# Weight sums and split feed-forward weights made beside the state space, one step per gate product, and GpSimd's sums moved to VectorE

## The chip, the core and the metric

The kernel runs on one core of a Trainium2 chip. Time is the device time of one execution, in microseconds (us). Five engines work from queues of their own, each in order: TensorE (PE in the profile; its weight loads are PEld), VectorE (DVE), ScalarE (ACT), GpSimd (POOL) and SyncE (SP), which only issues DMAs here. An instruction waits for semaphores, and everything behind it on its engine waits with it.

## What is computed

One decoder block over 1024 tokens of width 1024, in float32, with two branches, a mixer, a cross-attention into 256 memory tokens, and a feed-forward network of hidden width 2816:

```python
u = rms_norm(h, norm_mix[l])
proj = u @ w_in[l]
u_ssm, q, k, v, f_logit, gate_logits = jnp.split(proj, [...], axis=-1)
y_ssm = jax.nn.gelu(s5_ssm(u_ssm, ...))
glu_a, glu_b = jnp.split(y_ssm @ w_glu[l], 2, axis=-1)
out_a = glu_a * jax.nn.sigmoid(glu_b)
out_b = forgetting_attention(q, k, v, f_logit + b_forget[l]) @ w_fox_o[l]
gate_a, gate_b = jnp.split(jax.nn.sigmoid(gate_logits), 2, axis=-1)
h = h + (gate_a * out_a + gate_b * out_b) @ w_mix_out[l]
h = h + memory_cross_attention(rms_norm(h, norm_mem_q[l]), ...)
f_a, f_b = jnp.split(rms_norm(h, norm_ffn[l]) @ w_ffn_in[l], 2, axis=-1)
h = h + (jax.nn.silu(f_a) * f_b) @ w_ffn_out[l]
return rms_norm(h, norm_final)
```

## The kernel before

**Precision.** A float32 product is made of three products in fp32r: each operand is split into a high part (a cast by ScalarE) and a low part (source minus high, by VectorE, or by GpSimd where a flag says so). `split` (L175 to L178) does it; so casts stand at L177 and low parts at L178 for all callers.

**Seven products.** The mixer's product and the feed-forward products use a scheme of the Strassen kind on 2 x 2 blocks: seven block products in place of eight, at the price of sums and differences of blocks of both operands. The names S1 to S4, A11, A12 and A22 are such operands of the activations (h or l behind the name: high or low part); sums_d and w_d hold sums of weight blocks in DRAM.

**Stages, in the order of the span.** Up to about 115 us: load, normalise, transpose and project. About 117 to 330 us (`stage_ssm`): the state space, in four quarters q, among 32 gate products `gate(j, h)` of 24 matmuls each. A gate product ends in a sigmoid by ScalarE, and `mark` keeps these sigmoids. A dictionary `todo` says which step of the state space or of the mixer's weights stands ahead of which gate product; the program's order and a scheduler that looks at the queues make the order of each engine. For each quarter `xg` is read back from u_d, transposed data that the quarter's first products read; it is issued by SyncE, and so are the loads of raw weights, the stores y_d and the reads back of Ts. The block sums of w_mix_out are made here too (`mix_fetch`, `mix_sums`, `mix_store`, L490 to L505): two loads of 128x1024, four VectorE sums, four stores to sums_d, four times. About 330 to 620 us: the forgetting attention. About 620 to 820 us: the gated unit, `fox_part`, then the mixer's product (`mix_mm`, L615, and `mix_add`, L622, which adds a PSUM bank into the residual h on VectorE; the bank is free for its next product after that). Beside the mixer, a list `side` of small steps is worked off, one at a time: reads of S4, and the functions of `ahead(j)` for the feed-forward's first two weight blocks, j=0 and 1 (AHEAD_IN). `ahead` fetches 2 x 512 KB of w_ffn_in into wpr, makes five sums per block on GpSimd (L693 to L698), splits (wph, wpl), and stores seven tiles of 512 KB per block to w_d from ScalarE's queue (L671). About 820 to 945 us: cross-attention. From about 928 us: `norm_blocks(t)`, eight times, which normalises a token tile (the multiplier by `rstd`: VectorE, GpSimd, VectorE, L192 to L202), scales it into xs (L216, one buffer), transposes it on TensorE (L222) and, for t from 4 to 7, makes the operands S1 to S4 with the tile t-4 that it reads back from x_d as xa: two differences on VectorE (L877, L878), two on GpSimd (L879, L880), then splits, those of S2 with the low part on GpSimd. r_d keeps what makes S4 and A22 later. Then the feed-forward network: its input products (L961) from about 950 to 1395 us, the output products (L1098) from 1400 us.

`B.tc.issue_after(x)` makes the instructions of its body that run on the same engine as x, here ScalarE, come behind x in order.

## Time and profile before

| | us |
|---|---|
| median of three executions | 1608.38 (1606.6 to 1611.47) |
| the profiled execution | 1612.03 |
| its span | 1610.3 |
| its mean granted TensorE clock | 0.979 of full |

| engine | busy us | share |
|---|---|---|
| PE | 1539.8 | 96% |
| PEld | 1265.1 | 79% |
| DVE | 1071.1 | 67% |
| ACT | 670.9 | 42% |
| POOL | 282.9 | 18% |

The profile shows one execution. A row of the timeline or of the waits has the start in the span, the duration, the engine (SPq and ACTq: a DMA issue), the line, the operation, what it writes and reads, the shape, and in brackets how long the engine sat idle before it and what ended that. The DMA engines carry 161 GB/s on average, and 381 GB/s in the busiest of forty slices.

### The profile page before, as it was taken

To read this page: it belongs to the slowest core of one execution; us is meant where nothing else is said; L and a number is where in the kernel's file an instruction comes from. 1 tells how busy PE (TensorE), PEld (TensorE's weight loads), DVE (VectorE), ACT (ScalarE), POOL (GpSimd) and SP (SyncE) were. 2 spreads that over 40 slices of the span, in tenths; PEclk is the share of its full clock that TensorE was granted. 3 is DMA by queue.
4 is the path that set the end of the run, shared out by engine and by line. 5 is a ranking of instruction groups with operands and counts; after the bars stand their busy time and mean duration, and the time that the engine had idled before them with its cause. 6 is when DMAs were issued, how large, how long until landed. Compare 5 with 4: busy or idle time off the path is not lost.

```text
span 1610.3 us, 20551 instructions
## 1 busy us (share of the span) xinstructions
PE 1539.8 (96%) x7301; PEld 1265.1 (79%) x7301; DVE 1071.1 (67%) x1870; ACT 670.9 (42%) x1191; POOL 282.9 (18%) x353
## 2 busy tenths in 40 slices
PE   6899899999999899999899989999999999999997
PEld 5688788898777668887688767888888888788886
DVE  5758656434687777779665697677667776465555
ACT  5522333423566553233455564333333333244342
POOL 3024444010121124122202231001000000000001
PEclk8999999999999999999999999999999999999999
DMA  8747654552032736567632177444544454797642
GB/s 263 149 99 177 226 139 93 126 165 30 2 67 45 177 83 195 184 214 273 219 129 68 53 268 248 155 152 157 164 163 150 158 166 147 256 381 227 195 157 105
DMA packets 202871, 258.71 MB, mean 161 GB/s; under 512 B 36024, under 2 KB 127064, under 8 KB 202256
## 3 DMA queue, kind: packets, MB, share of 16 engines
q1 hardware_dynamic: 196144, 241.67, 50.2%
q10 hardware_dynamic: 6624, 15.73, 2.5%
q8 instruction: 57, 0.93, 0.2%
q14 instruction: 46, 0.38, 0.1%
HBM read 176.08 MB, written 83.20 MB: 161 GB/s over the span
## 4 chain that ended last, share of the span: by engine, by line
PE 76%; DVE 8%; DMA 5%; POOL 4%; issue 3%; ACT 2%; SPq 1%; DVEq 0%; POOLq 0%; ACTq 0%
PE mm L961 14%; PE pv L961 7%; PE mm L167 7%; PE mm L168 7%; PE mm L169 7%; PE mm L1098 4%; PE sc L961 3%; PE sc L1098 3%; PE pv L1098 3%; PE sc L167 2%; PE sc L169 2%; PE sc L168 2%; PE misc L1098 1%; DMA or<-in_w_ffn_out_dram 1%; PE pv L615 1%
## 5 line engine op out<-in xcount | busy, mean ns | idle before, releaser
L178 DVE TENSOR_TENSOR wlo<-raw,whi 128x1024 fp32r<-128x1024 f32 (+2 forms) x126 | 136.5, 1085 | 118.2 <-ACT whi L177 117.7
L177 ACT CAST whi<-raw 128x1024 fp32r<-128x1024 f32 (+2 forms) x127 | 115.6, 914 | 150.4 <-PE mm L168 41.7
L167 PE MATMUL mm<-uh,whi 128*128 128x512 f32 x344 | 138.2, 402 | 1.9 <-ACT whi L177 1.9
L178 DVE TENSOR_TENSOR ol<-or,oh 128x1024 fp32r<-128x1024 f32 x73 | 89.3, 1224 | 71.9 <-ACT oh L177 70.9
L169 PE MATMUL mm<-uh,wlo 128*128 128x512 f32 x344 | 136.1, 396 | 0.5 <-DVE wlo L178 0.5
L168 PE MATMUL mm<-ul,whi 128*128 128x512 f32 x344 | 135.8, 395 | 0.0
L177 ACT CAST oh<-or 128x1024 fp32r<-128x1024 f32 x73 | 76.8, 1052 | 104.5 <-PE mm L1098 34.8
L993 POOL TENSOR_TENSOR g<-a,c 128x512 f32<-128x512 f32 x22 | 35.6, 1616 | 381.6 <-ACT a L992 381.6
L1725 POOL TENSOR_TENSOR pl<-pf,ph 128x512 fp32r<-128x512 f32 (+1 forms) x32 | 39.5, 1235 | 225.8 <-DVE ph L1724 180.8
L169 PEld LDWEIGHTS mm<-uh,wlo 128*128 128x128 f32 x344 | 65.5, 190 | 15.0 <-DVE wlo L178 1.5
L167 PEld LDWEIGHTS mm<-uh,whi 128*128 128x128 f32 x344 | 65.8, 191 | 14.4 <-ACT whi L177 2.3
L168 PEld LDWEIGHTS mm<-ul,whi 128*128 128x128 f32 x344 | 65.6, 191 | 10.9
L196 POOL TENSOR_TENSOR r<-ms,mhalf 128x1 f32<-128x1 f32 (+1 forms) x30 | 20.5, 684 | 296.8 <-DVE ms L192 269.8
L1722 ACT ACTIVATE pf<-sc 128x512 f32<-128x512 f32 (+1 forms) x96 | 46.4, 490 | 49.6 <-DVE sc L1718 30.0
L961 PE MATMUL pv<-S3h,we 128*128 128x512 f32 x176 | 58.0, 391 | 1.1 <-ACT S3h L177 1.1
L1728 DVE TENSOR_TENSOR pl<-pf,ph 128x512 fp32r<-128x512 f32 (+2 forms) x64 | 35.6, 558 | 11.4 <-ACT ph L1727 10.7
L1193 POOL TENSOR_TENSOR sg<-sg,ga 128x512 f32<-128x512 f32 x16 | 28.4, 1801 | 73.2 <-DVE sg L1186 56.5
L167 PE MATMUL sc<-uh,whi 128*128 128x512 f32 x104 | 41.3, 397 | 0.0
L1098 PE MATMUL mm<-oh 128*128 128x512 f32 x106 | 41.2, 389 | 0.0
L1098 PE MATMUL mm<-ol,oh 128*128 128x512 f32 x106 | 41.2, 389 | 0.0
L1098 PE MATMUL mm<-oh,ol 128*128 128x512 f32 x106 | 41.2, 389 | 0.0
L167 PE MATMUL mm<-yh,whi 128*128 128x512 f32 x104 | 41.0, 394 | 0.0
(680 smaller groups left out, 4643.8 us busy)
## 6 DMA issues: line engine op xcount, KB each, us to landing
or<-c_d SPq DMA_DIRECT2D x77, 256.0 KB
wo<-in_w_ffn_out_dram SPq DMA_DIRECT2D x22, 512.0 KB
c_d<-g SPq DMA_DIRECT2D x44, 256.0 KB
t_d<-wo SPq DMA_DIRECT2D x44, 256.0 KB
or<-t_d SPq DMA_DIRECT2D x44, 256.0 KB
raw<-in_w_ffn_in_dram SPq DMA_DIRECT2D x20, 512.0 KB
rawb<-in_w_ffn_in_dram SPq DMA_DIRECT2D x20, 512.0 KB
raw<-in_w_in_dram SPq DMA_DIRECT2D x18, 512.0 KB
```

The lines of the kernel that those rows point to most:

```text
L167: T.matmul(ps, lh, rh, start=first, stop=False)
L168: T.matmul(ps, lh, rl, start=False, stop=False)
L169: T.matmul(ps, ll, rh, start=False, stop=last)
L177: self.A.copy(hi, src)
L178: (self.G if pool_lo else self.V).tensor_sub(lo, src, f32(hi))
L961: T.matmul(ps, l_[:, k, :], r_, start=first and k == 0 and i == 0, stop=k == 3 and i == 2, skip_group_check=True)
L993: G.tensor_mul(g[:, 512:], a1, c1)
L1098: T.matmul(ps, l_[:, gi], r_[:, 512:], start=n < 3 and p == 0 and k == 0 or n == 7 and p == 0 and k == 0, stop=p == NP - 1 and k == 2, ski ...
L1193: self.B.G.tensor_mul(self.out[j][:, cs], self.out[j][:, cs], ga)
L1722: self.exp = A.activation(pf[:, off:], ps[:, off:], AF.Exp)
L1725: G.tensor_sub(pl[:, off:], pf[:, off:], f32(ph[:, off:]))
L1728: V.tensor_sub(pl[:, off:], pf[:, off:], f32(ph[:, off:]))
```

## The change

It has five parts.

1. Tiles that prepare the state space come from the pool `sp` and no longer from `xin`, which is released when the first stage ends.
2. The split feed-forward weights of j=0 and 1 are made in `stage_ssm`. Each step is a job bound behind one gate product's sigmoid: the fetch at gate 15 + 8j, the seven parts at gates 16 + 8j to 22 + 8j in the order 1, 2, 5, 6, 7, 3, 4, and the stores of a part one gate later. Tiles are `wk` (128x1024, two buffers, shared with the mixer's sums) and `wh` (128x512, three buffers). Sums are on VectorE, and the stores to w_d go out from SyncE's queue, 14 of 256 KB per block.
3. The mixer's weight sums are such jobs too: fetch, sums and stores at gates 3 + 3k, 4 + 3k and 5 + 3k.
4. In `fox_part` the second difference of xm moves from GpSimd to VectorE, and S1 is split at once and no longer later (`late`). `side` keeps only the reads of S4.
5. In `norm_blocks` both sums and the low parts of S2 move from GpSimd to VectorE, S2 is put ahead of S3 and S1, and the sign of what r_d holds is turned, so that S4 needs no negation.

```diff
+    V, mw, kept = B.V, {}, {}
+    def wide():
+        return [qp.tile([P, D], F32, tag="wk", bufs=2, name="wk") for _ in range(2)]
...
+    def ffn_fetch(j):
+        mw["f", j] = wide()
+        for w_, c in zip(mw["f", j], (0, FH)):
+            S.dma_start(w_.rearrange("p (k c) -> p k c", k=8),
+                        w_ffn_in[:, c + j * P:c + (j + 1) * P].rearrange("(k p) c -> p k c", p=P))
+
+    def ffn_part(j, n):
+
+        (a1, a2), (b1, b2) = [(w_[:, :512], w_[:, 512:]) for w_ in mw["f", j]]
+        src, adds = {1: (a1, ()), 2: (a2, ()), 5: (a1, ((a2, b2), (a1, b1), (b1, b2))), 6: (a1, ((a2, a1), (a1, b2))),
+                     7: (b1, ()), 3: (b2, ()), 4: (a2, ())}[n]
+        for o, i in adds:
+            V.tensor_add(o, o, i)
+        kept[j, n] = [qp.tile([P, 512], F32R, tag="wh", bufs=3, name="wh") for _ in range(2)]
+        B.split(*kept[j, n], src)
+
+    def ffn_keep(j, n):
+        i, h = {1: (0, 0), 2: (0, 1), 5: (2, 0), 6: (2, 1), 7: (4, 0), 3: (5, 0), 4: (5, 1)}[n]
+        for m, t_ in enumerate(kept.pop((j, n))):
+            o = 512 * (m if n == 7 else h)
+            S.dma_start(w_d[j, i + (m if n != 7 else 0)][:, o:o + 512], f32(t_))
+
+    jobs = {}
+    for k in range(4):
+        for i, f in ((3 + 3 * k, mix_fetch), (4 + 3 * k, mix_sums), (5 + 3 * k, mix_store)):
+            jobs.setdefault(i, []).append(lambda f=f, k=k: f(k))
+    for j in range(AHEAD_IN):
+        jobs.setdefault(15 + 8 * j, []).append(lambda j=j: ffn_fetch(j))
+        for i, n in enumerate((1, 2, 5, 6, 7, 3, 4)):
+            jobs.setdefault(16 + 8 * j + i, []).append(lambda j=j, n=n: ffn_part(j, n))
+            jobs.setdefault(17 + 8 * j + i, []).insert(0, lambda j=j, n=n: ffn_keep(j, n))
...
-    for k in range(4):
-        for i, f in ((10 + 5 * k, mix_fetch), (12 + 5 * k, mix_sums), (13 + 5 * k, mix_store)):
-            todo.setdefault(i, []).append(lambda f=f, k=k: f(k))
...
         f()
+        if i in jobs:
+            with B.tc.issue_after(mark[-1].ins):
+                for g in jobs.pop(i):
+                    g()
...
-            if h and late:
-                late.pop(0)()
...
-        G.tensor_sub(x_[:, 512:], s1, x_[:, 512:])
+        V.tensor_sub(x_[:, 512:], s1, x_[:, 512:])
...
-        late.append(lambda: give("S1", bslot, k, x_[:, 512:]))
+        give("S1", bslot, k, x_[:, 512:])
...
-    side = [f for j in range(AHEAD_IN) for f in ahead(j)]
-    side[:0] = late + [lambda kk=kk: mix_s4(kk) for kk in range(2)]
+    side = [lambda kk=kk: mix_s4(kk) for kk in range(2)]
...
-        G.tensor_sub(a11, s1n, a11)
-        G.tensor_add(a12, a11, a12)
+        V.tensor_sub(a11, s1n, a11)
+        V.scalar_tensor_tensor(out=a12, in0=a11, scalar=-1.0, in1=a12, op0=ALU.mult, op1=ALU.subtract)
+        put("S2", slot, i, a11)
         put("S3", bslot, i, s3)
         put("S1", bslot, i, s1n, neg=True)
-        put("S2", slot, i, a11, low=G)
...
-        put("S4", bslot, i, y[:, :512], neg=True)
+        put("S4", bslot, i, y[:, :512])
```

What the engines' orders look like then is shown at three places; a row has the line, the operation, what it writes and reads, and the shape.

First SyncE in the second quarter of the state space, around the load of xg for q=1. Before:

```order
L505 DMA sums_d<-mw 128x512 x4
L492 DMA mw<-in_w_mix_out_dram 128x1024 x2
L153 DMA raw<-in_w_in_dram 128x4x256 x2
L505 DMA sums_d<-mw 128x512 x4
L1449 DMA xg<-u_d 128x1024
L1508 DMA y_d<-yh 128x1024
L1508 DMA y_d<-yl 128x1024
```

And with the change:

```order
L511 DMA sums_d<-wk 128x512 x4
L498 DMA wk<-in_w_mix_out_dram 128x1024 x2
L153 DMA raw<-in_w_in_dram 128x4x256 x2
L511 DMA sums_d<-wk 128x512 x4
L516 DMA wk<-in_w_ffn_in_dram 128x8x128
L1429 DMA xg<-u_d 128x1024
L516 DMA wk<-in_w_ffn_in_dram 128x8x128
L1488 DMA y_d<-yh 128x1024
L1488 DMA y_d<-yl 128x1024
```

A fetch of w_ffn_in now stands ahead of xg and another behind it; the mixer's sums keep their place.

Second VectorE in the mixer's product, where h is the residual (one name per token tile), raw and whi/wlo a mixer weight and its parts. Before:

```order
L622 TENSOR_TENSOR h_6963<-h_6963,mm 128x512
L178 TENSOR_TENSOR wpl<-wpr,wph 128x1024
L622 TENSOR_TENSOR h_6964<-h_6964,mm 128x512
L622 TENSOR_TENSOR h_6965<-h_6965,mm 128x512
L178 TENSOR_TENSOR wpl<-wpr,wph 128x512
L178 TENSOR_TENSOR wlo<-raw,whi 128x1024
L178 TENSOR_TENSOR wpl<-wpr,wph 128x512
L622 TENSOR_TENSOR h_6966<-h_6966,misc 128x512
L178 TENSOR_TENSOR wph<-wpr,wph 128x512
L622 TENSOR_TENSOR h_6959<-h_6959,mm 128x512
```

With the change, the same token tiles:

```order
L659 TENSOR_TENSOR h_7068<-h_7068,mm 128x512
L659 TENSOR_TENSOR h_7069<-h_7069,mm 128x512
L659 TENSOR_TENSOR h_7070<-h_7070,mm 128x512
L178 TENSOR_TENSOR wlo<-raw,whi 128x1024
L659 TENSOR_TENSOR h_7071<-h_7071,misc 128x512
L178 TENSOR_TENSOR wlo<-raw,whi 128x1024
L659 TENSOR_TENSOR h_7064<-h_7064,mm 128x512
L192 TENSOR_SCALAR ms_7339<-ss 128x1
L200 TENSOR_TENSOR rt_7341<-r_7340 128x1
```

The splits of the feed-forward weights are gone from between the additions; a chain for a multiplier (ms, r, rt) follows the first of the last four additions.

Third VectorE in the norm blocks of t=5 to 7 (s, sx: the differences; xs: the scaled tile; S1l, S2l, S3l: low parts). Before:

```order
L877 TENSOR_TENSOR s_8962<-xa,misc 128x512
L216 SCALAR_TENSOR_TENSOR xs<-h_6965,r_9024,gbc 128x1024
L878 TENSOR_TENSOR sx<-misc,sx 128x512
L178 TENSOR_TENSOR S3l<-s_8962,S3h 128x2x128 x2
L856 SCALAR_TENSOR_TENSOR S1l<-sx,S1h 128x2x128 x2
L192 TENSOR_SCALAR ms_9074<-ss 128x1
L200 TENSOR_TENSOR rt_9076<-r_9075 128x1
L201 SCALAR_TENSOR_TENSOR rt_9076<-rt_9076,ms_9074 128x1
L202 SCALAR_TENSOR_TENSOR r_9075<-rt_9076,r_9075 128x1
L970 TENSOR_TENSOR a_9003<-a_9003,sc 128x512
L216 SCALAR_TENSOR_TENSOR xs<-h_6966,r_9075,gbc 128x1024
```

With the change, from the second half of the same block (its s, sx, first sum and first S3l stand ahead):

```order
L862 SCALAR_TENSOR_TENSOR xa<-xa 128x512
L178 TENSOR_TENSOR S2l<-xa,S2h 128x2x128 x2
L178 TENSOR_TENSOR S3l<-s_8994,S3h 128x2x128
L838 SCALAR_TENSOR_TENSOR S1l<-sx,S1h 128x2x128 x2
L200 TENSOR_TENSOR rt_9057<-r_9056 128x1
L192 TENSOR_SCALAR ms_9106<-ss 128x1
L201 SCALAR_TENSOR_TENSOR rt_9057<-rt_9057,ms_9055 128x1
L202 SCALAR_TENSOR_TENSOR r_9056<-rt_9057,r_9056 128x1
L200 TENSOR_TENSOR rt_9108<-r_9107 128x1
L952 TENSOR_TENSOR a_9035<-a_9035,sc 128x512
L216 SCALAR_TENSOR_TENSOR xs<-h_7070,r_9056,gbc 128x1024
```

The xs of t=6 stood right behind s of t=5; now all operands of t=5 stand ahead of it.

More of the change, by code (lines that the diff above doesn't have):

```diff
@@ L288, in sincos @@
         return sn, cs, s
+AHEAD_IN = 2
 @with_exitstack
@@ L319, in hybrid_block_kernel @@
         with tc.tile_pool(name="qp", bufs=1, reuse_waits="tile") as qp:
-            stage_ssm(B, s5, qp, uT, w_in, gate_d, u_d, y_d, w_mix_out, sums_d)
+            stage_ssm(B, s5, qp, uT, w_in, gate_d, u_d, y_d, w_mix_out, sums_d, w_ffn_in, w_d)
     yT = Act(big, "big", 16, 4, L, name="y")
@@ L454, in stage_in, with stage_ssm @@
         acts[step[0]](step[1:])
-def stage_ssm(B, s5, qp, uT, w_in, gate_d, u_d, y_d, w_mix_out, sums_d):
+def stage_ssm(B, s5, qp, uT, w_in, gate_d, u_d, y_d, w_mix_out, sums_d, w_ffn_in, w_d):
     A, S = B.A, B.S
@@ L546, in stage_tail @@
     s3_d = B.dram.tile([2, P, D], F32, name="s3_d")
-    fox, part, xm, mixw, msets, late = {}, {}, {}, {}, [], []
+    fox, part, xm, mixw, msets = {}, {}, {}, {}, []
     def operand(name, mk):
```

81 lines of the change are left out of this document (17 added, 64 removed).

## The prediction

> **What bounds the kernel now.** I read the page first, for the engine shares and the chain that ended last.
>
> ```profile
> span 1610.3 us, 20551 instructions
> PE 1539.8 (96%) x7301; PEld 1265.1 (79%) x7301; DVE 1071.1 (67%) x1870; ACT 670.9 (42%) x1191; POOL 282.9 (18%) x353
> PE 76%; DVE 8%; DMA 5%; POOL 4%; issue 3%; ACT 2%; SPq 1%; DVEq 0%; POOLq 0%; ACTq 0%
> ```
>
> TensorE is busy for 1539.8 of 1610.3 us and the change adds or removes no matmul, so it can only win back some of the 70 us in which TensorE stands still, and the slow matmuls behind such stops. Next come the windows over the stretches in which the change works, with one undisturbed stretch as a measure.
>
> ```profile
> 185.00:200.00 15.00, 12.79 (x73) 11.05 (x72) 9.15 (x15) 8.28 (x13) 4.56 (x6) 0.95 0.97 304
> 230.00:335.00 105.00, 105.00 (x559) 90.44 (x558) 46.09 (x66) 38.07 (x60) 21.76 (x45) 1.00 0.58 131
> 737.00:800.00 63.00, 55.20 (x228) 43.53 (x227) 50.70 (x74) 25.95 (x45) 21.75 (x15) 0.95 0.76 269
> 940.00:960.00 20.00, 15.58 (x81) 12.93 (x80) 18.89 (x32) 10.34 (x27) 10.02 (x10) 0.99 0.79 282
> 960.00:980.00 20.00, 15.34 (x50) 11.18 (x51) 14.52 (x17) 7.84 (x18) 8.91 (x8) 0.76 0.85 299
> ```
>
> Columns: length, busy time of PE, PEld, DVE, ACT and POOL, granted clock, DMA share, GB/s. From 230 to 335, where the new feed-forward work goes, TensorE never stops and VectorE is 44% busy (46.09 of 105). From 737 to 800, which that work leaves, TensorE lacks 7.8 us; from 940 to 980, where GpSimd's sums go to VectorE, 9.1 us. The list of TensorE's waits, kept to 737 to 800 (three rows) and to 950 to 983 (four), names them:
>
> ```profile
> PE misc L615 <- DVE h L622: 2.6, 1, 2.6
> PE mm L615 <- DVE h L622: 2.2, 2, 1.4
> PE misc L222 <- DVE h L622: 2.2, 1, 2.2
> PE pv L222 <- DVE xs L216: 6.2, 1, 6.2
> PE mm L961 <- POOL S2l L178: 1.3, 1, 1.3
> PE pv L961 <- ACT S3h L177: 1.1, 1, 1.1
> PE mm L961 <- ACT S2h L177: 0.4, 1, 0.4
> ```
>
> So the mix stage loses 7.0 us on additions that VectorE makes late, the norm stage 9.0.
>
> **Part 1, the mix stage is freed of the prepared weights.** The timeline of ScalarE, VectorE, GpSimd and TensorE there, in this order, shows why an addition of 0.68 us comes late.
>
> ```profile
> 771.31 1.05 ACT L177 CAST whi<-raw 128x1024 fp32r<-128x1024 f32 x1 [4.66 <-DMA raw<-in_w_mix_out_dram]
> 783.40 1.14 ACT L177 CAST wph<-wpr 128x512 fp32r<-128x512 f32 x2 [3.72 <-POOL wpr L698]
> 774.17 1.23 DVE L178 TENSOR_TENSOR wpl<-wpr,wph 128x1024 fp32r<-128x1024 f32 x1
> 784.05 0.69 DVE L178 TENSOR_TENSOR wpl<-wpr,wph 128x512 fp32r<-128x512 f32 x1 [1.82 <-ACT wph L177]
> 784.66 0.68 DVE L622 TENSOR_TENSOR h<-h,misc 128x512 f32<-128x512 f32 x1
> 781.23 2.14 POOL L698 TENSOR_TENSOR wpr<-wpr 128x512 f32<-128x512 f32 x1
> 785.39 0.62 PE L615 MATMUL misc<-whi,S4h 128*128 128x512 f32 x1 [2.62 <-DVE h L622]
> 785.81 0.63 PE L615 MATMUL misc<-wlo,S4h 128*128 128x512 f32 x1
> ```
>
> The addition into h at 784.66 stands in VectorE's queue behind a split into wpl that waits for ScalarE's cast, which waits for GpSimd's sum, 2.14 us long. In the changed order none of the three is left here. The earlier wait (1.36 us at 774) stands behind a mixer weight split whose raw weight came late (4.66 us) while w_d stores and w_ffn_in loads filled the queues; those go too. After a stop, matmuls follow each other 0.42 us apart (785.39, 785.81), where an undisturbed gate product of 24 takes 5.44 us (the sigmoids behind two of them, quoted in part 3, start at 263.79 and 269.23), 0.227 each. The window's granted clock, 0.95, says what that costs: 0.05 x 63 = 3.2 us, which I put half behind the stop of 2.6 us and half behind that of 2.2. So 7.0 of waits and 3.2 of clock, 10.2 us, hang on this. The four subtractions xm that come from GpSimd to VectorE cost 4 x 0.68 = 2.7 us of an engine idle for 12.3 of 63 us, beside matmuls. What stays: the addition into misc that was waited for at 795 stands behind two rstd chains in the new order, about 1 us. **Term: -9** (bounds: -4, if only the wait at 785 and its clock go; -11, if all goes).
>
> The Trainium skill, "TensorE: Matmul & The Clock Gate", section "What's actually happening", says that the clock halves only after an idle window of about 3.4 us. Here matmuls ran at the slow pace after stops of 2.6 and 2.2 us, so the measurement decides; by the page the slow matmuls would have another cause and need not go, and the term would be -5.8.
>
> **Part 2, the norm blocks' sums on VectorE.** The timeline of before, VectorE, GpSimd, SyncE and TensorE in this order:
>
> ```profile
> 949.91 0.41 DVE L856 SCALAR_TENSOR_TENSOR S1l<-sx,S1h 128x256 fp32r<-128x256 f32 x1
> 952.24 1.28 DVE L216 SCALAR_TENSOR_TENSOR xs<-h,r,gbc 128x1024 f32<-128x1024 f32 x1
> 955.79 2.35 DVE L856 SCALAR_TENSOR_TENSOR S1l<-sx,S1h 128x256 fp32r<-128x256 f32 x2
> 960.36 1.28 DVE L216 SCALAR_TENSOR_TENSOR xs<-h,r,gbc 128x1024 f32<-128x1024 f32 x1
> 970.70 0.69 DVE L877 TENSOR_TENSOR s<-xa,misc 128x512 f32<-128x512 f32 x1 [3.81 <-DMA xa<-x_d]
> 974.85 1.78 POOL L178 TENSOR_TENSOR S2l<-xa,S2h 128x256 fp32r<-128x256 f32 x2
> 966.13 0.42 SPq L874 DMA_DIRECT2D xa<-x_d  x1
> 954.98 0.60 PE L222 MATMUL pv<-ident,xs 128*128 128x128 f32 x4
> 961.79 1.08 PE L222 MATMUL pv<-ident,xs 128*128 128x128 f32 x4 [6.21 <-DVE xs L216]
> ```
>
> Per block VectorE gains two sums of 512 (2 x 0.6) and two splits of 256 (2 x 0.37): 2.0 us. It gets about as much back, since a 256-wide operation took 0.41 alone but 1.18 (2.35 for two) beside GpSimd's, and four of them stand in each block. So its load stays level, and GpSimd's chain of 1.4 + 1.3 + 1.8 us (S2l ends it at 974.85) goes from the path to the S2 matmuls.
>
> Against this, the order changes: the multiplier and xs of t=6 stood just behind s of t=5, and now come behind its sx, two sums, S3l, S2l and S1l: 0.6 + 2 x 0.6 + 6 x 0.37 + 1.1 for the small chain and a, 5.1 us, and 0.9 more for the block before. xs(6) slips from 952.24 to some 958; its transposes, which were running at 954.98 in before, wait to about 959. Then s(6), which reads them, stands ahead of xs(7), so xs(7) runs near 961 instead of 960.36. The 6.2 us wait is split in two and not shortened: **+0.5**.
>
> After it the gain comes. The load of xa for t=7 (966.13) was queued behind the store of r_d, which holds GpSimd's second sum; in the new order it stands ahead of that store, and can be issued some 4 us earlier, so s(7) no longer waits 3.8 us; and S2l is no longer late. The waits 1.3 + 1.1 + 0.4 = 2.8 go. The clock of 0.76 from 960 to 980 costs 0.24 x 20 = 4.8 us; a third of it, 1.6, I put behind these waits, the rest stays behind the wait for xs. So -4.4. **Term: -4** (bounds: 0, if xs(7) comes 4 us later; -9, if its wait goes too). VectorE's order is what is late next.
>
> **Part 3, the state space stage takes the work.** Its rows: SyncE, TensorE, VectorE, ScalarE.
>
> ```profile
> 189.95 0.79 SPq L1449 DMA_DIRECT2D xg<-u_d  x1
> 272.57 0.43 SPq L1449 DMA_DIRECT2D xg<-u_d  x1
> 286.64 13.67 SPq L1438 DMA_DIRECT2D Ts<-Ts  x3
> 197.60 2.91 PE L1456 MATMUL pv<-xg,F 128*128 128x128 f32 x16 [2.21 <-DMA xg<-u_d]
> 291.63 1.61 PE L1456 MATMUL pv<-xg,F 128*128 128x128 f32 x13
> 270.41 0.29 DVE L1406 TENSOR_TENSOR d<-EC,trg_cs 128x128 f32<-128x128 f32 x1 [6.81 <-POOL ES L1408]
> 263.79 0.60 ACT L476 ACTIVATE gs<-mm 128x512 f32<-128x512 f32 x1 [4.84 <-PE mm L169]
> 269.23 0.60 ACT L476 ACTIVATE gs<-sc 128x512 f32<-128x512 f32 x1 [3.91 <-PE sc L169]
> ```
>
> Added are 14 casts (14 x 0.6 = 8.4 us) and 24 VectorE operations of 512 (24 x 0.68 = 16.3 us). They lie mostly within 230 to 335, where VectorE has 59 us free and TensorE does not wait: no cost by themselves. The cover is a gate product of 5.44 us (263.79 to 269.23) in each of several banks; it goes where a cast holds up the sigmoids behind it by about three products, 16 us.
>
> The loads in SyncE's queue cost something. The xg load for q=1 was the one that TensorE waited for (2.21 us), and the new order puts a fetch of w_ffn_in ahead of it. That fetch is 0.5 MB, at the 304 GB/s of this window 1.7 us, and waits for the last store of sums from its buffer: issue about 1 us later. So 2.7 us later at most, and up to 1.6 of slow matmuls more, as behind a stop of the mix stage. The xg load for q=3 (272.57, needed at 291.63) comes behind the second block's fetch, whose buffers are free after the last split of the first, near 280; landing near 288 leaves 3 us. **Term: +3.5** (bounds: 0, if the queue takes the fetch between others; +8, if q=3 waits too). w_d is read again at about 950, so the stores, 28 of 256 KB instead of 14 of 512, have 600 us.
>
> **Sum.** -9 - 4 + 3.5 = -9.5 from the profiled execution's 1612.0: 1602.5. That execution lies 3.65 above the median of 1608.38, so **1599 us** on that footing.
>
> **Rivals.** (A) Slower: ScalarE's queue in the state space stage. A cast of wh needs one of three buffers, each freed by a store in SyncE's queue; a store behind Ts, which held the queue for 13.7 us at 286.64, and a split behind VectorE's 6.8 us wait at 270.41 together hold the cast for 20.5 us, and the sigmoid behind it too. Beyond 16 us the banks are full: 4.5 us of TensorE for each block plus 1.6 of clock, 12.2 for two. With xg at both places late (the bound of +8) the stage costs 20 us against gains of 13: +7, 1615 us. It decides from three products upward. For it: all four queues are in order, and the new work passes each of them. Against it: the two waits lie 9 us apart at different parts, and the 20.5 needs both in one. Chance 0.14.
> (B) The norm blocks gain nothing, as VectorE in series is as late as GpSimd beside it: -5.5, 1603 us. For it, the split wait above. Chance 0.20.
> (C) In the mix stage only the wait at 785 goes (-4), the others stay with the late mixer weight and the rstd chains: -4.5, 1604 us. Chance 0.15.
> That the change doesn't move what it says is excluded by the order of both.
>
> **How the numbers follow.** The forecast has 0.51. About 0.3%, 4.8 us, is what a measurement can tell here, so faster means under 1603.6, slower over 1613.2. Forecast 0.50 faster; B and C stand on the edge, half of each faster (0.17), half within; A is mostly slower. Faster 0.66, same 0.21, slower 0.13. The range goes from all good bounds (-11 - 9 + 0 = -20, 1588) to all bad ones (-4 + 0 + 8 = +4, 1612); what it leaves out is most of A and little else.
>
> **What would show it.** Part 1: waits on h in the mix stage below 2 us, clock 1.0. Part 2: two waits on xs of 4 and 1 us, none on S2l. Part 3: the first wait on xg at 4 to 5 us; none at q=3; no wait of a gate product on a sigmoid. Wrong it is if sigmoids hold TensorE in 230 to 335, or if the feed-forward stage, which I leave untouched, changes.

## The result, and the profile after

The changed kernel is a little slower: median 1619.92 us (1617.77 to 1623.4, seven runs) against 1611.47 (1606.03 to 1614.66, seven runs) of the kernel before; the ratio is 1.0057 with a 95% interval of 1.0036 to 1.0078, or 9.2 us. The forecast was 9.4 us the other way. The page of the profile after, its span, TensorE's row and the chain that ended last:

```profile
span 1616.1 us, 20580 instructions
PE 1538.5 (95%) x7301; PEld 1267.2 (78%) x7301; DVE 1071.5 (66%) x1902; ACT 670.2 (41%) x1193; POOL 237.7 (15%) x323
PE 73%; DVE 9%; DMA 8%; POOL 3%; ACT 3%; issue 3%; SPq 1%; DVEq 0%; POOLq 0%; ACTq 0%
```

TensorE's busy time is as before (1538.5 against 1539.8), so the whole difference is standing still; GpSimd has 45 us less to do (237.7 against 282.9), and in the chain DMA has grown from 5% to 8%. The windows of after over the five stretches of the prediction, in its columns (length, busy time of PE, PEld, DVE, ACT and POOL, granted clock, DMA share, GB/s):

```profile
185.00:200.00 15.00, 11.17 (x62) 9.29 (x60) 8.76 (x13) 8.15 (x12) 5.45 (x6) 0.96 0.82 221
230.00:335.00 105.00, 94.51 (x462) 79.88 (x460) 56.07 (x89) 34.70 (x60) 22.78 (x48) 0.95 0.61 154
737.00:800.00 63.00, 63.00 (x279) 52.18 (x278) 49.36 (x72) 22.13 (x31) 1.69 (x1) 1.00 0.63 217
940.00:960.00 20.00, 20.00 (x108) 16.50 (x107) 17.15 (x39) 14.30 (x38) 1.06 (x2) 1.00 0.70 236
960.00:980.00 20.00, 15.66 (x71) 12.81 (x69) 17.49 (x39) 11.48 (x31) 1.48 (x2) 0.84 0.89 312
```

The mix stage (737 to 800) is now full at full clock, and the norm stage (940 to 980) stands 4.3 us where it stood 9.1. But 230 to 335, which was full before, now lacks 10.5 us. The windows stand at the same times and not over the same work, since after runs 16 to 27 us behind in the last three; moved along with the work they say the same (764 to 817 is full at clock 1.00, 956 to 996 stands 4.3 us). All of TensorE's waits of after from 115 to 350 us (total, times, longest):

```profile
PE pv L1479 <- ACT Tt L1423: 11.3, 3, 6.8
PE pv L1436 <- DMA xg<-u_d: 6.6, 1, 6.6
PE pv L1405 <- ACT m L1483: 6.5, 1, 6.5
```

That is 24.4 us. Before, the list for this stage has two rows:

```profile
PE pv L1456 <- DMA xg<-u_d: 2.2, 1, 2.2
PE pv L1499 <- ACT Tt L1443: 2.1, 1, 2.1
```

So 20.1 us of waits are new. To count a stage with its slow matmuls I take the **lag**: the start of a certain matmul in the profile after less the start of the same matmul before. The state space runs from its first product with xg to the first attention product; in the timeline of before and then of after these start at

```profile
145.03 0.38 PE L1456 MATMUL pv<-xg,F 128*128 128x128 f32 x2
411.08 0.40 PE L1740 MATMUL pv<-ph,vhi 128*65 128x512 f32 x1
```

```profile
144.96 0.50 PE L1436 MATMUL pv<-xg,F 128*128 128x128 f32 x3
436.34 0.39 PE L1720 MATMUL pv<-ph,vhi 128*65 128x512 f32 x1
```

The lag grows from -0.1 to 25.3: **the state space loses 25.3 us**. Taken in the same way at the later stages, the attention adds 2.0, the mix stage gives back 11.0, the norm stage 6.9 and the feed-forward 3.3, which leaves 6.0; the spans differ by 5.8. So the profiled pair stands a little closer than the timed runs. Lags of one pair of profiles are good to some 2 us: the first stage, which no kernel here changes, differs by -1 to +4, and e4, which leaves the state space as before, reads -2.2 there.

What is left in the mix and norm stages is in TensorE's waits of after, first from 737 to 850, then from 950 to 1010:

```profile
PE misc L222 <- DVE u2l L178: 1.3, 1, 1.3
PE misc L222 <- DVE rt L201: 3.1, 1, 3.1
PE mm L943 <- DMA whi<-w_d: 1.2, 1, 1.2
```

No wait on h, none on S2, and instead of 6.2 us for xs one of 3.1 us for the multiplier's chain (rt).

**Where the 25.3 us come from.** The timeline of after around the wait of 6.5 us, VectorE, SyncE, ScalarE and TensorE in this order:

```profile
278.45 0.29 DVE L1386 TENSOR_TENSOR d<-EC,trg_cs 128x128 f32<-128x128 f32 x1 [6.81 <-POOL ES L1388]
280.20 1.22 DVE L178 TENSOR_TENSOR wlo<-raw,whi 128x1024 fp32r<-128x1024 f32 x1
281.74 0.68 DVE L178 TENSOR_TENSOR wh<-wk,wh 128x512 fp32r<-128x512 f32 x1
280.11 1.72 SPq L153 DMA_DIRECT2D raw<-in_w_in_dram  x2
282.45 4.48 SPq L533 DMA_DIRECT2D w_d<-wh  x3
294.00 0.62 ACT L177 CAST wh<-wk 128x512 fp32r<-128x512 f32 x1 [18.14 <-DMA w_d<-wh]
295.93 1.09 ACT L1483 ACTIVATE m<-pv 128x512 f32<-128x512 f32 x2
296.67 1.09 PE L1405 MATMUL pv<-ident,fre 128*128 128x128 f32 x4 [6.51 <-ACT m L1483]
```

VectorE stands 6.8 us for GpSimd, a wait that was there before. Behind it stand the splits that free raw and fill wh. SyncE's queue holds the loads of raw and then the stores of wh; these go out from 282.45, and the cast at 294.00 has waited 18.14 us for one of the three wh buffers. Behind that cast stands m, and TensorE waits for m. The 18.14 us begin at 275.86: 2.6 us of them are the end of VectorE's wait for GpSimd, 4.0 the splits until the first of these stores is issued, and 11.5 the time from there until the cast can start. Some 50 us on, in the same order of engines but SyncE first:

```profile
303.42 1.07 SPq L533 DMA_DIRECT2D w_d<-wh  x2
305.54 18.21 SPq L1418 DMA_DIRECT2D Ts<-Ts  x3
323.85 16.43 SPq L533 DMA_DIRECT2D w_d<-wh  x8
320.50 0.69 DVE L178 TENSOR_TENSOR wh<-wk,wh 128x512 fp32r<-128x512 f32 x1 [14.86 <-DMA w_d<-wh]
336.26 0.62 ACT L177 CAST wh<-wk 128x512 fp32r<-128x512 f32 x1 [12.82 <-DVE wk L525]
338.08 1.04 ACT L1423 COPY Tt<-Ts 128x1024 f32<-128x1024 f32 x1
339.18 0.79 PE L1479 MATMUL pv<-xg,Tt 128*128 128x128 f32 x2 [6.84 <-ACT Tt L1423]
```

VectorE's split at 320.50 waits 14.86 us for a buffer, whose store was issued at 303.42 or just behind and took some 16 us to land; the next stores stand behind three Ts reads that hold SyncE's queue for 18.2 us. With VectorE held, the state space's operations behind the split are late too, and the sum that the cast at 336.26 needs stands behind them; Tt stands behind the cast, and TensorE waits for Tt. It reads as one loop through four in-order queues: cast, buffer, store, queue, and again the engines that feed the cast.

### The profile page after: what moved, and what is told of

It is laid out like the page before. It is cut to its first block, busy times and chain, and to the rows that moved or that the text cites. A ratio compares the mean times of both kernels' runs of the same rounds, so it can differ in the third digit from the quotient of the medians.

```text
span 1616.1 us, 20580 instructions
## 1 busy us (share of the span) xinstructions
PE 1538.5 (95%) x7301; PEld 1267.2 (78%) x7301; DVE 1071.5 (66%) x1902; ACT 670.2 (41%) x1193; POOL 237.7 (15%) x323
## 4 chain that ended last, share of the span: by engine, by line
PE 73%; DVE 9%; DMA 8%; POOL 3%; ACT 3%; issue 3%; SPq 1%; DVEq 0%; POOLq 0%; ACTq 0%
PE mm L943 15%; PE pv L943 7%; PE mm L167 6%; PE mm L169 6%; PE mm L168 6%; PE mm L1080 4%; PE sc L943 4%; PE sc L1080 3%; PE pv L1080 3%; DMA w_d<-wh 2%; PE mm L652 2%; PE sc L167 2%; PE sc L169 2%; PE sc L168 2%; PE misc L1080 1%
## 5 line engine op out<-in xcount | busy, mean ns | idle before, releaser
L169 PE MATMUL sc<-uh,wlo 128*128 128x512 f32 x104 | 41.0, 394 | 0.0
L168 PE MATMUL sc<-ul,whi 128*128 128x512 f32 x104 | 41.0, 394 | 0.0
```

Of the source, the lines that this page charges most:

```text
L168: T.matmul(ps, lh, rl, start=False, stop=False)
L169: T.matmul(ps, ll, rh, start=False, stop=last)
```

## The experiments

Four theories were set against each other: the buffers (a cast of wh without a buffer stops ScalarE), SyncE's queue (the fetch ahead of xg, the stores among raw, Ts and xg), the DMA traffic itself, and the mere amount of added work on VectorE and ScalarE. All results in one table: the loss of the state space in us by lags (in brackets up to q=1, from there to q=3, and from there to the attention), and the ratio to the kernel before with its interval (without one: a single time, whose scatter is some 0.3%).

| run | loss in the state space | ratio to before |
|---|---|---|
| after | 25.3 (5.2, 11.9, 8.3) | 1.0057 [1.0036, 1.0078] |
| e1_no_ffn_prep | 1.8 (1.8, 0, 0) | 0.9895 [0.987, 0.9919] |
| e2_seven_buffers | 21.8 (4.6, 4.2, 13.0) | 1.0041 [1.0025, 1.0057] |
| e3_xg_first | 24.9 (2.5, 14.4, 7.9) | 1620.23 us |
| e5_no_stores | 12.6 (5.5, 2.4, 4.6) | 0.9997 [0.9977, 1.0017] |
| e6_no_splits | 11.2 (10.9, 0.2, 0) | 1605.79 us |
| e7_act_stores | 21.8 (1.2, 12.2, 8.4) | 1.0041 [1.0019, 1.0062] |
| e8_one_block | 15.6 (3.1, 14.0, -1.5) | 1610.11 us |
| e9_casts_on_vector | 25.0 (7.3, 16.0, 1.7) | 1.0052 [1.0033, 1.0071] |
| e10_unbound | 19.2 (11.3, 8.1, -0.2) | 1.003 [1.0011, 1.0048] |
| e11_casts_three_buffers | 25.7 (10.7, 16.6, -1.5) | 1620.31 us |
| e12_engine_work_only | 8.9 (0, 2.1, 6.9) | 1602.43 us |
| e13_fetches_only | 7.8 (6.8, 0.9, 0) | 1600.00 us |
| e14_gpsimd_stores | 2.7 (2.3, 0.2, 0.1) | 0.9921 [0.9894, 0.9948] |
| e15_merged_stores | 14.2 (1.4, 4.6, 8.2) | 0.9993 [0.9975, 1.001] |
| e16_one_word | 25.8 (5.7, 21.6, -1.5) | 1.0077 [1.0052, 1.0101] |
| e17_sums_too | 12.1 (10.7, 0.8, 0.6) | 0.9985 [0.9969, 1.0002] |
| e18_gate_stores_gpsimd | 18.4 (11.3, 5.4, 1.7) | 1613.23 us |

The medians of before in these groups are 1608.46 to 1611.16 us.

**Which part of the change costs, and which gain.** e1 takes the feed-forward jobs out of the state space and fills w_d with raw weights, so that the feed-forward product has the same transfers:

```diff
-    for j in range(AHEAD_IN):
+    for j in range(0):
...
+    for j in range(AHEAD_IN):
+        for i in range(7):
+            S.dma_start(w_d[j, i], w_ffn_in[i * P:(i + 1) * P, j * D:(j + 1) * D])
```

> Edit: the changed kernel, but the state space stage makes no feed-forward weights (no fetch, sums, splits or stores of j=0, 1); w_d is filled with raw pieces of w_ffn_in by 14 plain DRAM copies behind the last gate product, so the sums and splits of these two weight blocks are left out. Theory 1 (the whole loss sits in the prepared weights' way through the state space stage, and the gains further on are real): TensorE's lag against before is 0 to 2 us at the end of the state space (it was 25), the mix stage gives back 10 and the norm stage 7 to 10 as in the changed kernel; about 17 us under before, ratio 0.989. Rival (the gains further on are a loan: the DMAs and weights there were early only because TensorE was 25 us late): the mix and norm stages give back less than 8 us together; ratio 0.995 to 1.0.

Measured: a loss of 1.8 us and a ratio of 0.9895. The feed-forward jobs are the loss, and the mixer's jobs, bound to gates too, are not. The mix stage gains 10.5 us and the norm stage 6.5, nearly as in after.

e4 is the kernel before with part 5 of the change alone:

```diff
-        G.tensor_sub(a11, s1n, a11)
-        G.tensor_add(a12, a11, a12)
+        V.tensor_sub(a11, s1n, a11)
+        V.scalar_tensor_tensor(out=a12, in0=a11, scalar=-1.0, in1=a12, op0=ALU.mult, op1=ALU.subtract)
+        put("S2", slot, i, a11)
...
-        put("S2", slot, i, a11, low=G)
...
-        put("S4", bslot, i, y[:, :512], neg=True)
+        put("S4", bslot, i, y[:, :512])
```

> Edit: the kernel before with the norm blocks' part of the change alone (both sums and the low parts of S2 on VectorE, S2 put first, no negation of S4). Theory (it is worth by itself what the changed kernel shows there, a lag that falls by 10 us from 954 to 982 after rising by 3 before): 7 us under before, ratio 0.995 to 0.997. Rival (it gains only where the mix stage leaves VectorE, GpSimd and the DMAs ahead of time): ratio 0.999 to 1.001. My forecast had 4 us for it.

Measured: 0.9965 [0.9947, 0.9983], 5.6 us faster; the norm stage by 6.1, the feed-forward behind it by 3.5, the mix stage by nothing (+0.4). So the norm blocks' gain is their own.

**Buffers, order of xg, and both with another queue.** e2 gives wh seven buffers; for their room preparation tiles go back to the first stage's pool (not shown):

```diff
-        kept[j, n] = [qp.tile([P, 512], F32R, tag="wh", bufs=3, name="wh") for _ in range(2)]
+        kept[j, n] = [qp.tile([P, 512], F32R, tag="wh", bufs=7, name="wh") for _ in range(2)]
```

> Edit: the changed kernel with seven buffers of wh in place of three; the room comes from putting the state space's preparation tiles back into the first stage's pool, as before. Same instructions, same order of SyncE's queue. Theory 1 (a cast of wh waits for a buffer that a store further back in SyncE's queue must free, and holds up the sigmoids and the copies of Tt behind it): no cast waits for w_d any more, TensorE's waits on Tt and m in 230 to 345 us (17.8 us) go, the lag at the end of the state space falls from 25 to about 7 (the late xg of q=1 stays), total 1 to 2 us under to 10 us under before, ratio 0.993 to 0.999. Rival (what costs is the amount of work added on VectorE and ScalarE and the DMA traffic, wherever it waits): the lag stays at 20 or more, ratio 1.003 to 1.006.

Measured: 21.8 us, so the buffers alone bring 3.5. TensorE's waits of e2 from 115 to 350 us, and the longest one of the casts:

```profile
PE pv L1481 <- ACT Tt L1425: 12.6, 2, 9.9
PE pv L1438 <- DMA xg<-u_d: 9.8, 2, 6.2
ACT wh L177 <- DVE wk L526: 11.2, 1, 11.2
```

No cast waits for a store any more; the cast waits for VectorE's sum instead, and xg is now late twice. The theory of the buffers alone has fallen.

e3 issues the fetch of w_ffn_in behind the load of xg:

```diff
-        S.dma_start(self.xg, u_d[q].rearrange("t (n g) c -> (t n) g c", g=8))
+        self.xgd = S.dma_start(self.xg, u_d[q].rearrange("t (n g) c -> (t n) g c", g=8))
...
+        with B.tc.issue_after(s5.xgd.ins):
```

> Edit: the changed kernel with the first block's fetches of w_ffn_in bound behind the load of xg for q=1 in SyncE's queue, all else in the same order. Theory (the fetch, which waits for the stores of the mixer's sums to land, holds up xg): TensorE's wait on xg falls from 6.6 to about 2.2 us, the lag at 203 us from 5.1 to about 1, and the total by 4 to 5 us; the later stalls stay. Rival (the window's DMA traffic, 0.97 busy, makes xg late, not the queue): the wait stays above 5 us.

Measured: 24.9; up to q=1 it loses 2.5 instead of 5.2, and gives it back later. e7 has the edits of e2 and e3, and the stores of wh go out from ScalarE's queue (`A.dma_start(w_d...)`):

> Edit: the changed kernel with three mends at once: seven buffers of wh, the first block's fetches behind the load of xg for q=1, and the stores to w_d issued from ScalarE's queue (each one gate after its part, as now), so that SyncE's queue holds none. Nothing is left out. Theory 1: lag at the end of the state space 3 to 7, total 8 to 13 us under before, ratio 0.992 to 0.995. Rival 2 (engine work) and rival 3 (DMA traffic): lag 15 to 20, ratio 1.000 to 1.004.

Measured: 21.8. The stores now stand in the queue of the very engine whose casts they free, and the loss after q=1 is as in after (20.6 against 20.1). TensorE waits 18.1 us for Tt, in three times. ScalarE's timeline of e7 at one of them:

```profile
277.68 0.33 ACTq L535 DMA_DIRECT2D w_d<-wh  x1
278.05 0.62 ACT L177 CAST wh<-wk 128x512 fp32r<-128x512 f32 x1 [9.69 <-DVE ES L1391]
```

ScalarE's own store of wh stands ahead of the cast and waits for VectorE's split, and Tt stands behind the cast. So in this queue ScalarE is held by its stores.

**What of the work costs.** e5 keeps fetches, sums and splits and drops the stores (the jobs `ffn_keep`); w_d is filled as in e1.

> Edit: the changed kernel without the 28 stores of wh to w_d in the state space stage (fetches, sums, casts and subtractions stay; w_d is filled with raw pieces of w_ffn_in by plain DRAM copies behind the last gate product, so the prepared weights are not used). Theory 1, widened after the run with seven buffers (it freed the casts from the buffers and the lag fell only from 25 to 20, while copies of Ts and the xg of q=3 still came late in SyncE's queue): the stores in SyncE's in-order queue, each waiting for a cast or subtraction, hold back Ts and xg behind them, and their landing holds the wh buffers. Then the lag at the end of the state space falls to 5 to 9 (xg of q=1 stays late), and the total is 8 to 12 us under before. Rival 2 (VectorE's and ScalarE's added operations, in order with the state space's own, cost the time): the lag stays at 15 to 20. Rival 3 (DMA traffic in these windows): in between, 10 to 14, since 7 of 11 MB go.

e6 keeps fetches and stores and drops sums and splits, so the raw parts are stored:

```diff
-        for o, i in adds:
-            V.tensor_add(o, o, i)
-        kept[j, n] = [qp.tile([P, 512], F32R, tag="wh", bufs=3, name="wh") for _ in range(2)]
-        B.split(*kept[j, n], src)
+        kept[j, n] = [src, src]
```

> Edit: the changed kernel without the sums, casts and subtractions of the feed-forward weights in the state space stage; fetches and the 28 stores stay, which now store raw halves of wk (so the sums and splits are left out). The counterpart of the run without stores. As nothing ties the stores to the gates, SyncE takes them in two clumps, early. Theory 1 (stores that wait for a cast or subtraction are what holds the queue): nothing waits, lag 3 to 8 at the end of the state space. Rival 2 (engine work): the same, 3 to 8. Rival 3 (DMA traffic and number of DMAs): the lag stays above 12.

e12 keeps sums and splits, but on the mixer's tile, without fetches and stores; e13 keeps the fetches alone. Both fill w_d as in e1.

> Edit: the changed kernel with only the engine work of the feed-forward weights in the state space stage: the same sums, bound casts and subtractions at the same gates, but on the mixer's last pair of wk, which is there already, with no fetches and no stores (w_d is filled with raw pieces by plain copies behind the last gate product). Rival 2 (engine work in order with the state space's chain): lag at the end of the state space 10 or more. If the DMAs are the cause (3 or 4): 1 to 4.

> Edit: the changed kernel with only the four fetches of w_ffn_in in the state space stage, no sums, casts, subtractions or stores (w_d is filled with raw pieces behind the last gate product). Rival 3 (the fetches in 512-byte pieces fill the DMA engines): lag 5 at q=1, as in the changed kernel, and 3 or more at q=2 or q=3 besides. If they cost only where they stand ahead of xg for q=1: 5 there and nothing after. If nothing without the rest: 1 to 2.

Measured: work without transfers loses 8.9, with the fetches 12.6, with the stores too 25.3, against 1.8 without all of it. So the stores are half of the loss (12.7), though ScalarE and VectorE do nothing for a store. The fetches alone lose 7.8, of it 6.8 up to q=1, where the fetch stands ahead of xg. e6 loses 11.2, of it 10.9 up to q=1, where TensorE waits 12.7 us for ScalarE's copy into F (the last section shows it): later nothing is lost once sums, casts and splits are gone.

e8 prepares block j=0 alone (j=1 filled as in e1).

> Edit: the changed kernel with only the first of the two weight blocks made in the state space stage; the place of the second in w_d is filled with raw pieces by plain copies at the stage's end, so its sums and splits are left out. In the changed kernel the lag was 5 at 203 us, 6 at 275, 16 at 303 and 25 at 341, and the second block's parts start at about 300. Theory 1: the first block's part of the lag, 13 to 17, stays and the second's 8 to 10 goes. If instead the lag is set by the end of the stage (both blocks' work has to fit between 236 us and the end), it is below 8.

Measured: 15.6, of it 14.0 from q=1 to q=3: half of the work has more than half of the loss.

**The casts, and the binding.** e9 has the edits of e2 and e3, and makes the high part on VectorE; e11 does so on after, with three buffers:

```diff
-        B.split(*kept[j, n], src)
+        hi, lo = kept[j, n]
+        V.tensor_copy(hi, src)
+        V.tensor_sub(lo, src, f32(hi))
```

> Edit: the changed kernel with seven buffers of wh, the first block's fetches behind the load of xg for q=1, and the casts to wh on VectorE in place of ScalarE, so that ScalarE's queue holds nothing of the feed-forward weights; stores stay in SyncE's queue. Nothing is left out. So far: without the stores the lag over the state space is 12, without sums, casts and subtractions (but with all stores) it is 0 after q=1, and with the stores in ScalarE's queue and free buffers it is still 21. Theory 1 as it now stands (the casts in ScalarE's in-order queue are the lock: each waits for a buffer, or for VectorE's sum, which itself stands behind the state space's chain on VectorE, and the copies of Tt, m and the sigmoids wait behind the cast): with no cast on ScalarE the lag at the end of the state space is 2 to 6, the total 11 to 15 us under before, ratio 0.990 to 0.994. Rival 2 (VectorE's added work): 14 operations more on VectorE, so the lag is 21 or more, ratio above 1.004. Rival 4 (stores that wait in SyncE's queue between the steps of Ts): as in the run without stores against that with seven buffers, the lag is still 10 or more.

> Edit: the changed kernel with the casts to wh on VectorE and nothing else (three buffers, fetch ahead of xg for q=1, stores from SyncE). Theory 1: now a full set of buffers holds VectorE, not ScalarE, and VectorE feeds the state space's chain: lag 5 at q=1, and 8 to 15 at the end, between the changed kernel (25) and the run with seven buffers and casts on VectorE. If the buffers don't matter once ScalarE is free: 5 to 7 at the end.

Measured: 25.0 and 25.7. ScalarE is free of the casts and nothing is won. The size is what the rival "more work on VectorE" forecast, but TensorE's waits of e9 from 115 to 350 us are for ScalarE again; below them is ScalarE's timeline at one of them:

```profile
PE pv L1441 <- ACT F L1411: 20.4, 3, 9.0
PE pv L1484 <- ACT Tt L1428: 3.3, 1, 3.3
```

```profile
261.00 0.33 ACTq L481 DMA_DIRECT2D gate_d<-gs  x1
261.37 0.58 ACT L1411 COPY F<-pv 128x512 f32<-128x512 f32 x1 [7.13 <-DMA y_d<-yh]
```

The copy into F stands behind ScalarE's own issue of gate_d, which waits until a store of y_d that SyncE issued has landed (the last section has more on this). In e11 it is the same: 16.4 of 23.9 us are waits for F, and one copy stood 13.19 us for a store of y_d. So the hold stays on ScalarE and moves to another instruction. e10 has the edits of e2 and e3, and its jobs stand in the program's order without `issue_after`.

> Edit: as the run with casts on VectorE (seven buffers, xg for q=1 first, stores from SyncE), but the casts stay on ScalarE, and the jobs are not bound behind the gates' sigmoids; the scheduler places the casts, earlier than the bound ones. The order of SyncE's queue is nearly that of the run with casts on VectorE. If the cast's place on ScalarE is the lock whatever its binding: lag 10 to 20, well above that run. If the binding to late gates is what makes the casts collide (parts at gates 16 to 31, while data is there from about 205 us): lag 2 to 6, like that run.

Measured: 19.2. Without the binding two casts stand so early in ScalarE's queue that they wait 12.0 and 17.4 us for the fetch; F stands behind them, and 17.3 us of TensorE's waits are for F. So taking the binding away doesn't take the loss away; that the binding has no part in after's loss isn't shown.

**The stores' queue.** e14 has the edits of e2 and e3, and the stores go out from GpSimd's queue. It leaves nothing out:

```diff
-            S.dma_start(w_d[j, i + (m if n != 7 else 0)][:, o:o + 512], f32(t_))
+            B.G.dma_start(w_d[j, i + (m if n != 7 else 0)][:, o:o + 512], f32(t_))
```

> Edit: the changed kernel with seven buffers of wh, the first fetches behind xg for q=1, and the stores to w_d issued from GpSimd's queue, whose DMAs have semaphores of their own; nothing is left out. Theory 4 (stores in SyncE's queue and the shared semaphores of hardware DMAs): the lag at the end falls to 3 to 8, ratio 0.991 to 0.996. Rival 5 (GpSimd, which makes EC and ES in small steps in order, now waits at each store for VectorE): the lag is 15 or more, with VectorE's waits on ES above 7 us.

Measured: 2.7 us lost instead of 25.3, and 0.9921 [0.9894, 0.9948]: median 1594.65 against 1610.05 us. **This version beats both kernels.** Its mix stage gains 10.5 and its norm stage 6.5, nearly as in after. TensorE's waits of e14 from 115 to 350 us:

```profile
PE pv L1482 <- ACT Tt L1426: 4.0, 2, 2.7
PE pv L1439 <- ACT F L1409: 3.9, 1, 3.9
```

7.9 us instead of 24.4. The window from 250 to 340 us, first of after, then of e14:

```profile
250.00:340.00 90.00, 75.33 (x359) 63.52 (x358) 49.49 (x75) 30.58 (x53) 17.64 (x40) 0.92 0.59 148
```

```profile
250.00:340.00 90.00, 88.77 (x467) 75.77 (x466) 55.98 (x80) 40.41 (x66) 30.98 (x63) 1.00 0.78 203
```

e14 moves more bytes in this window (203 against 148 GB/s), its DMA engines are busier, its VectorE and ScalarE do more, and TensorE stands 1.2 us instead of 14.7. So neither the traffic nor the amount of work has to cost 25 us. They aren't free in every order either: e12 has the same sums and splits without transfers and loses 8.9, with waits for Tt and F. My reading is that what decides is which instructions come to stand behind one that waits.

e16 changes this one word in after and nothing else:

> Edit: the changed kernel with the 28 stores of w_d issued from GpSimd's queue in place of SyncE's; nothing else (three buffers of wh, fetch ahead of xg for q=1), nothing left out. Theory 4 (the stores' queue and semaphores are the cause, buffers and the order at q=1 are small): lag 5 at q=1 from the fetch, 5 to 9 at the end; ratio 0.993 to 0.997. Rival 1 (with three buffers the casts still wait, now for a store in GpSimd's queue): 12 or more, ratio above 0.999.

Measured: 25.8 us, 1.0077. The queue alone brings nothing. ScalarE in the timeline of e16:

```profile
293.79 0.62 ACT L177 CAST wh<-wk 128x512 fp32r<-128x512 f32 x1 [19.98 <-DVE d L1387]
294.32 1.04 ACT L1423 COPY Tt<-Ts 128x1024 f32<-128x1024 f32 x1
```

A cast still waits 20 us (the profile puts it down to VectorE), Tt still stands behind it, and TensorE waits 18.4 us for Tt.

e15 has the edits of e2 and e3 but for the buffers: three of 128x1024, and half as many stores of twice the size from SyncE. e17 is e14 with the stores of sums_d on GpSimd's queue too; e18 is e2 and e3 with the stores gate_d on it and those of wh on SyncE's.

> Edit: the changed kernel with high and low part in one wh tile of 128x1024 (three buffers, the room of six before) and one store for both: 14 stores of 512 KB in place of 28 of 256; the first fetches behind xg for q=1. Nothing is left out. Theory 4 (number of DMAs that share eight semaphores): the lag at the end falls from 20 to 8 to 14, ratio 0.996 to 1.000. Rival 2 or 3: 18 to 22, as with seven buffers.

> Edit: the kernel of e14 (stores of w_d from GpSimd, seven buffers, xg for q=1 ahead of the fetch), and the mixer's 16 stores of sums_d from GpSimd's queue too; nothing left out. If the same cause also makes the 2 to 3 us at q=0 and q=1 that are left: lag 0 to 1, total 2 us under e14, ratio 0.989 to 0.992. If not, as e14 (0.992), or worse where GpSimd's steps of EC and ES wait for VectorE's sums at 170 to 200 us.

> Edit: the changed kernel with seven buffers, the first fetches behind xg for q=1, the w_d stores on SyncE as in the changed kernel, and the 32 gate_d stores issued from GpSimd's queue, so that ScalarE issues no DMA in the state space stage and can't be held at one; nothing left out. If ScalarE's wait at its own DMA issues, for a semaphore that a late DMA of SyncE holds, is the main part: lag 2 to 7 at the end. If the stores' place in SyncE's queue, ahead of Ts, xg and raw weights, is the main part: lag 14 to 21, with TensorE's waits on Tt and xg.

Measured: 14.2, 12.1 and 18.4. The version with fewer and larger stores in SyncE's queue loses less than e2; more stores on GpSimd's do harm (e17 against e14: 8.4 us more up to q=1, which I can't explain in detail). e18's size and its waits, Tt 11.3 us and xg 8.7, are what it forecast for the stores' place in SyncE's queue. But 11.3 of its loss lie up to q=1, where the sigmoids' stores come to stand in GpSimd's queue and a sigmoid waits 10.81 us for one (at 189.82), so it doesn't tell what it was made for.

**What follows.** Seven buffers alone bring 3.5, xg first alone 0.4, the stores' queue alone -0.5; the three together 22.6. Seven buffers and xg first, run with the stores on ScalarE's queue, still lose 21.8. I read the locks as standing in series: whichever is opened alone, the next one holds ScalarE's copies. That buffers alone, the order of xg alone and the queue alone don't do it is shown, and so is that moving the stores to ScalarE's queue doesn't. Not run were e2 and e3 together with the stores left on SyncE's queue, and e14 without xg first. After q=1, e2 loses 17.2 us and e14 0.4, so buffers on SyncE's queue don't make the later quarters whole; the part of xg's order is open.

## Why the prediction was wrong

**Part 1, the mix stage: right.** Forecast -9, measured -11.0 in after and -10.5 in e1 and e14. No wait on h, clock 1.00, as foretold; the good bound of -11 was the truth, so the wait behind the rstd chains, put at 1 us, didn't come.

By the rule of the Trainium skill, "TensorE: Matmul & The Clock Gate", section "What's actually happening", the term would have been -5.8; the stops went, the clock went from 0.95 to 1.00 and the stage gained all of it. That agrees with the rows, not with that reading of the rule.

**Part 2, the norm blocks: right in kind.** Forecast -4, measured -6.9, and -6.1 alone (e4). The part on S2 and xa went as said. Mis-sized was the term "+0.5": xs waits were to be 4 and 1 us, and there is one of 3.1, for rt. VectorE got its time back for the sums, as foretold: a pair of S1l took 2.35 us in before, beside GpSimd's sums, and takes less than a third of it in after, where GpSimd has none there:

```profile
980.72 0.75 DVE L838 SCALAR_TENSOR_TENSOR S1l<-sx,S1h 128x256 fp32r<-128x256 f32 x2
```

(The 0.41 us that the prediction took as the time of one alone, at 949.91, lay beside GpSimd's S2l of 949.04 to 950.91, so it was thin proof; the row above is better.) Rival B, no gain, is excluded by e4.

**Part 3, the state space: wrong.** Forecast +3.5 with +8 as its worst bound, measured +25.3. The xg term was about right: 6.6 us instead of 4 to 5 at q=1, none at q=3, and up to q=1 the lag is 5.2. What failed is the step "no cost by themselves. The cover is a gate product of 5.44 us (263.79 to 269.23) in each of several banks". That cover holds for sigmoids, and indeed no gate product waited for one. But ScalarE's queue holds two other kinds of instruction, the copies into Tt and m, for which TensorE has no spare at all: 17.8 of the 24.4 us of waits are theirs. The point from which a held cast costs was put at 16 us; for Tt and m it is the next use. Left out beside it was the time that a store takes from its issue until its buffer is free: the 11.5 us of the first wait and some 16 us of the second. The prediction gave the stores 600 us, until w_d is read again, and no time at all to free wh.

**Rival A** had the loop (three buffers, SyncE's queue, VectorE's wait for GpSimd, the cast). That its 20.5 us lie near the 18.14 measured is chance: the 20.5 was 13.7 us of Ts in SyncE's queue and 6.8 of VectorE's wait, and in the 18.14 there is no wait behind Ts (those reads come only at 305.54, when that cast is done), but the time until a store landed. It was given 0.14 because "the two waits lie 9 us apart at different parts, and the 20.5 needs both in one". The waits were taken as fixed in time. My reading of the rows is that they aren't: a store that is late behind one makes the cast late, the cast makes the split late, and the chain comes to the second wait as well. The price of A, 20 us, was near the 25.3 measured; on the prediction's footing its 1615 us compares with 1608.38 x 1.0057 = 1617.5. But that price came from sigmoids with full banks, and no gate product waited for a sigmoid, so the nearness is luck too. Its named lock, ScalarE's cast, was one of several: without it (e9, e11) the loss was as large, at the copies into F.

**The feed-forward stage**, said to be untouched, gained 3.3 us; e4 gained 3.5 there, e1 lost 0.5, so only that it comes and goes between runs is shown. The 2.0 us of the attention stay open, and so does how much of part 3's loss each single queue has.

## What to carry to other kernels

Work that is put beside a tight stage is not free because engines are idle and the bound engine has a cover: list every kind of instruction that stands behind the new one in its queue, and take the cover of the one with the least. Count the engine's own DMA issues among them. Where new work runs in a ring (cast, buffer, store, queue, cast), its waits can add up though they lie apart, the time until a store lands is one of them, and widening one link can move the hold to the next; change the buffers and the queue of the stores together and look at the lag of the stage. Idle shares and DMA shares said nothing here: the version with more traffic and more work in the same 90 us was the one that didn't stop.

## What the hardware showed beside that

**A DMA issue on one queue waits for a DMA of another.** TensorE's longest wait in e6 and ScalarE's timeline there:

```profile
PE pv L1433 <- ACT F L1403: 12.7, 1, 12.7
```

```profile
206.84 0.33 ACTq L480 DMA_DIRECT2D gate_d<-gs  x1
207.21 0.59 ACT L1403 COPY F<-pv 128x512 f32<-128x512 f32 x1 [9.08 <-DMA w_d<-wk]
```

ScalarE's copy into F reads no weight, yet it stood 9.08 us until a store of w_d, issued by SyncE, had landed: ahead of it in ScalarE's queue was its own issue of gate_d. In the program each DMA issue of SyncE and ScalarE takes one of eight semaphores that they share, and waits until that one's last transfer is done; GpSimd's have eight of their own. In the program of e6, the issue of gate_d in this row waits for the semaphore that SyncE's store of w_d raises; e9 and e11 show the same with stores of y_d. So the hold is there; how much of after's 25.3 us it has is open. It would also be a reason why GpSimd's queue did what ScalarE's didn't (e14 against e7), but in e7 ScalarE stood at its own stores as well, and e18, which was to show it, adds holds of its own, so that stays argued.

The Trainium skill, "DMA: Bandwidth & Descriptors", section "Issuing engines are not separate DMA queues", says that DMAs run on the same 16 DMA engines whichever engine issues them, and that issuing from several engines only saves the sequencer's issue time. Here the loss went from 21.8 us (e7) to 2.7 (e14) for the same stores, twice what 28 issues take (0.33 us each in most rows here, some 9 us): as I read it, what counted was who stands behind a store that has to wait.

**Full DMA engines, few bytes.** The window of 18 us in which the casts of after waited longest:

```profile
278.00:296.00 18.00, 12.16 (x60) 9.92 (x58) 7.84 (x17) 1.97 (x3) 0.45 (x3) 0.95 0.84 136
```

The DMA engines are 84% busy at 136 GB/s, where before, from 185 to 200, 97% moved 304. What runs here are loads of w_in and w_ffn_in in pieces of 1 KB and 512 bytes: the three stores issued from 282.45 to 286.93 had to share with them.
